# The Toeplitz stage of a hybrid state-space and attention layer in steps of four groups

## The chip, the cores and the metric

The kernel runs on one core of a Trainium2 chip. The metric is the device time of one execution in microseconds (us). A core has five engines that matter here: TensorE (PE in the profile, with its weight loads as PEld), VectorE (DVE), ScalarE (ACT), GpSimd (POOL) and SyncE (SP, which here only issues transfers). Each works through its own queue of instructions in order; they wait for each other through semaphores. Sixteen DMA engines move data between the chip's memory (DRAM) and the on-chip SBUF; transfers are issued from the queues of SP, ACT and POOL. TensorE writes its results to PSUM, in banks of 128 x 512 numbers of 32 bits.

## What is computed

One encoder layer over two sequences of 512 tokens with 1024 channels: an S5 state-space branch and a windowed attention branch are gated and added, then comes a squared-ReLU MLP. The change is in the S5 branch, which for 64 groups of 16 channels runs a complex linear recurrence of 64 states forward and backward and reads the states out:

```python
def one_direction(us, d, reverse):
    bu_re = jnp.einsum('lgc,gpc->lgp', us, bb_re[d])
    bu_im = jnp.einsum('lgc,gpc->lgp', us, bb_im[d])
    ...
    _, _, h_re, h_im = lax.associative_scan(_complex_combine, (ar, ai, bu_re, bu_im),
                                            reverse=reverse, axis=0)
    return (jnp.einsum('lgp,gcp->lgc', h_re, cr[d])
            - jnp.einsum('lgp,gcp->lgc', h_im, ci[d]))

y = one_direction(ug, 0, False) + one_direction(ug, 1, True)
y = jax.nn.gelu(y + dsk * uf)
return y * jax.nn.sigmoid(y @ w_glu + b_glu)
```

Queries, keys, values, the branch's input `u` and two gates come from one projection `h @ w_in`. Everything is in 32-bit floating point.

## The kernel before

**The recurrence in chunks.** A sequence is cut into 64 chunks of T = 8 tokens (NCHUNK = 64). Inside a chunk the output is a Toeplitz product of the inputs; between chunks a state `h` is handed on by a scan of 62 iterations on DVE (L600 to L606). The output of a group is then three products that add up in one area of 128 x 128 in PSUM: the Toeplitz matrix `toep` by the input `u_sb` (L642), and the table `ctab` (real and imaginary part) by the chunk states `st` (L645).

**The tables stage before it** (`tables`, L464 to L566) makes for every four groups a table of nine powers, 9 x 16 columns for each part, and writes it to DRAM (`ct_scr`, L522, from POOL's queue). The ninth power serves only the lag products of that stage; the Toeplitz stage uses the first T x 16 columns. `toep_scr` is written in DRAM as well (L576).

**The Toeplitz stage** (L594 to L668) takes the 64 groups in 32 steps q of two groups (SH = 2). The order of a step is written out by hand for TensorE, ACT and DVE (`manual_schedule`, L599: these three run in the order of the program); POOL and SP are placed by a planner. In step q:

1. TensorE: products of both groups into one PSUM bank `ps` from a pool of two banks (`sps`, L639 to L646).
2. The state copies for step q + 2 (`state_rows`, L609 to L618): rows 64 to 127 on DVE, rows 0 to 63 on ACT for an even q and on DVE for an odd one; three buffers of tag `st`.
3. DVE: `remainder()` of step q - 1, the lower part `ylo` = `yg` - `yhi` (L622).
4. In every second step ACT issues the two stores of the four groups before (`store_y`, L626: `yhi`, then `ylo`).
5. ACT: GELU of the bank into `yg` (L655) and its rounding `yhi` (L621).
6. `pull(n)`: filler matmuls, see below.
7. POOL: the loads of a new table every four groups (`load_table`, L590, three buffers) and of `u_sb` and `toep` every eight groups (`load_batch`, L582 and L584, two buffers each).

A bank is written again two steps later, and only when the GELU has read it.

**Fillers.** While DVE and ACT do the scan and these steps, TensorE works off other products of the layer: `pull(n)` (L260) takes matmuls from a generator until n units are used up. First come 24 columns of the projection (`products` and `column`, L180 to L212; each in two halves, one for a sequence, of 24 matmuls, two units a matmul), then eight key tiles (`key_products`, L214 to L239; 24 matmuls of one unit each). Together that is 2 x 3 x 8 x 2 x 24 + 3 x 8 x 8 = 2496 units. What belongs to a product is written into the queues at the place where it is pulled:

- the last matmul of a half brings `finish`: ACT copies the result out of PSUM (L200 here), and after a column's second half ACT issues its store (L209);
- the 4th and the 10th matmul of a column's first half, and the 3rd and the 7th of the first key tile, bring `split`: ACT rounds a piece of the next weights to `c_hi` (L175), DVE makes the remainder `c_lo` (L176);
- the last matmul of a key tile brings a chain: square on ACT (L232), sum on DVE (L234), addition and power on POOL (L236, L237), multiplication on DVE (L238).

In the Toeplitz stage the units that are left are spread evenly over the steps (L660), but for 84, which are pulled after its end (L667) before the attention begins with `w_lo` (L981) and its first product (L813).

```python
pull(32)                                             # L608
...
pull(-(-(phase["units"] - 84) // (GROUPS // SH - q)))  # L660
```

Of the kernel before, what the change touches and what calls it, by code (L numbers as in the profile page):

```python
# [12 lines left out]
F32 = mybir.dt.float32  # L13
F32R = mybir.dt.float32r
I32 = mybir.dt.int32
AF = mybir.ActivationFunctionType
# [3 lines left out]
P = 128  # L20
# [5 lines left out]
NSEQ = 2  # L26
# [12 lines left out]
GROUPS = 64  # L39
STATE = 64  # L40
CH = 16
T = 8
NCHUNK = SEQ // T
SB = 8
SI = 4
SG = 4
SH = 2
# [16 lines left out]
def hybrid_layer(ctx, tc, x, rel, onehot, w_qkv, w_ug, vectors, lam, coefs, w_glu, w_out, ln2,  # L64
                 w_up, w_down, out):
    nc = tc.nc
    V, S, PE, GP, SP = nc.vector, nc.scalar, nc.tensor, nc.gpsimd, nc.sync
# [4 lines left out]
    dram = ctx.enter_context(tc.tile_pool(name="dram", bufs=1, space=DRAM))  # L72
# [22 lines left out]
    ga_scr = dram.tile([KT, P, NTOK], F32, name="ga_scr")  # L95
# [55 lines left out]
    phase = {"next": 0, "raw": [], "units": 2 * 3 * KT * NSEQ * len(columns) + 3 * KT * NT, "gelu": False}  # L151
# [119 lines left out]
    with tc.tile_pool(name="xin", bufs=1, reuse_waits="tile") as xin, tc.tile_pool(name="ssmc", bufs=1) as sc:  # L271
# [148 lines left out]
        ps = ps_o.tile([P, 512], F32, tag="po", name="line")  # L420
# [21 lines left out]
    with tc.tile_pool(name="hst", bufs=1) as hp:  # L442
# [11 lines left out]
        with tc.tile_pool(name="ssmt", bufs=2) as sp:  # L454
# [9 lines left out]
            def tables(c):  # L464
# [22 lines left out]
                for q in range(SB // SG):  # L487
                    g0 = c * SB + q * SG
# [20 lines left out]
                    for ri, t in enumerate((bi_p, br_p)):  # L509
# [5 lines left out]
                    ctab = sp.tile([P, SG, 2, 9, CH], F32, tag="ctab", name="ctab")  # L515
# [3 lines left out]
                    V.tensor_sub(ctab[:, :, 0], tb, ctab[:, :, 0])  # L519
                    V.tensor_mul(ctab[:, :, 1], bc_pow(er, 9), bc_ch(cw[:, 1], 9))  # L520
                    V.tensor_sub(ctab[:, :, 1], ctab[:, :, 1], tb)
                    GP.dma_start(ct_scr[:, g0:g0 + SG].rearrange("p g r n -> p (g r n)"),  # L522
                                 ctab.rearrange("p g r n c -> p (g r n c)"))


                    u_sb = sp.tile([P, SI, NSEQ * NCHUNK], F32, tag="u_sb", name="u_sb", bufs=1)
                    SP.dma_start(u_sb, u_scr[g0:g0 + SI].rearrange("g c t k -> (c t) g k"))
                    bms = []
                    for gp in range(SG // SH):
                        bm = sp.tile([P, 2, SH, P], F32, tag="bm", name="bm")  # L530
                        bms.append(bm)
                        ps = tps()
# [45 lines left out]
        with tc.tile_pool(name="ssmo", bufs=2) as sp:  # L578
            def load_batch(g0):

                u_sb = sp.tile([P, SB, NSEQ * NCHUNK], F32, tag="u_sb", name="u_sb")
                GP.dma_start(u_sb, u_scr[g0:g0 + SB].rearrange("g c t k -> (c t) g k"))  # L582
                toep = sp.tile([P, SB, T, CH], F32, tag="toep", name="toep")
                GP.dma_start(toep.rearrange("p g t c -> p g (t c)"),  # L584
                             toep_scr[:, :, g0:g0 + SB].rearrange("c t g n -> (c t) g n"))
                return u_sb, toep

            def load_table(g0):
                ctab = sp.tile([P, SI, 2, 9 * CH], F32, tag="ctab", name="ctab_in", bufs=3)
                GP.dma_start(ctab.rearrange("p g r n -> p (g r n)"),  # L590
                             ct_scr[:, g0:g0 + SI].rearrange("p g r n -> p (g r n)"))
                return ctab

            ahead = [load_batch(0)]  # L594
            ahead_c = [load_table(0), load_table(SI), load_table(2 * SI)]
            ahead.append(load_batch(SB))
            GP.dma_start(line_scr, line_one[:, None, :].to_broadcast([N_HEADS, P, LINE]))
            order.close()
            order.enter_context(tc.manual_schedule(engines={mybir.EngineType.PE, mybir.EngineType.Activation, mybir.EngineType.DVE}))  # L599
            for i in range(1, NCHUNK - 1):  # L600
                t1, t2 = [sp.tile([P, 2, GROUPS, NSEQ], F32, tag="st", name=n, bufs=3) for n in ("t1", "t2")]
                V.tensor_mul(t1, h[:, i], a8r)
                V.tensor_mul(t2, h[:, i, ::-1], a8i)
                V.tensor_add(t1, t1, h[:, i + 1])
                V.tensor_add(h[:, i + 1], t1, t2)
                pull(15)  # L606
            phase["gelu"] = True
            pull(32)  # L608
            def state_rows(q):  # L609
                st = sp.tile([P, 2, SH, NSEQ, NCHUNK], F32, tag="st", name="st", bufs=3)  # L610
                hv = h[:, :, :, q * SH:(q + 1) * SH, :].rearrange("p k r g s -> p r (g s) k")
                sv = st.rearrange("p r g s k -> p r (g s) k")
                V.tensor_copy(sv[64:128], hv[64:128, :, :, ::-1])
                if q % 2 == 0:
                    S.copy(sv[0:64], hv[0:64])
                else:
                    V.tensor_copy(sv[0:64], hv[0:64])
                return st  # L618

            def rounded(y, parts, g):  # L620
                S.copy(parts[0][:, g:g + SH, :], y)  # L621
                return lambda: V.tensor_sub(parts[1][:, g:g + SH, :], y, parts[0][:, g:g + SH, :].bitcast(F32))  # L622

            def store_y(parts, ga):
                for e in range(2):
                    S.dma_start(y_scr[e, :, :, ga:ga + SI].rearrange("t c g k -> (t c) (g k)"),  # L626
                                parts[e].rearrange("p g k -> p (g k)").bitcast(F32))

            states = [state_rows(0), state_rows(1)]
            remainder = full = None  # L630
            for q in range(GROUPS // SH):
                g0 = q * SH
                if g0 % SB == 0:
                    u_sb, toep = ahead.pop(0)
                if g0 % SI == 0:
                    ctab = ahead_c.pop(0)
                    ysp = [sp.tile([P, SI, NSEQ * NCHUNK], F32R, tag=f"y{n}", name=f"y{n}") for n in ("hi", "lo")]
                st = states.pop(0)
                ps = sps()  # L639
                for g in range(SH):  # L640
                    o = ps[:, g * P:(g + 1) * P]
                    PE.matmul(o, toep[:, g0 % SB + g].rearrange("p t c -> p (t c)"), u_sb[:, g0 % SB + g, :],  # L642
                              start=True, stop=False)
                    for ri in range(2):
                        PE.matmul(o, ctab[:, g0 % SI + g, ri, 0:T * CH],  # L645
                                  st[:, ri, g].rearrange("p s k -> p (s k)"), start=False, stop=ri == 1)  # L646
                if q + 2 < GROUPS // SH:
                    states.append(state_rows(q + 2))
                if remainder:
                    remainder()  # L650
                if full:
                    store_y(*full)
                    full = None
                yg = sp.tile([P, SH, NSEQ * NCHUNK], F32, tag="yg", name="yg")
                S.activation(yg.rearrange("p g k -> p (g k)"), ps[:, 0:SH * P], AF.Gelu_apprx_tanh)  # L655
                remainder = rounded(yg, ysp, g0 % SI)
                if (g0 + SH) % SI == 0:
                    full = ysp, g0 + SH - SI

                pull(-(-(phase["units"] - 84) // (GROUPS // SH - q)))  # L660
                if (g0 + SH) % SI == 0 and g0 + SH + 2 * SI < GROUPS:
                    ahead_c.append(load_table(g0 + SH + 2 * SI))
                if (g0 + SH) % SB == 0 and g0 + SH + SB < GROUPS:
                    ahead.append(load_batch(g0 + SH + SB))
            remainder()
            store_y(*full)
            pull(phase["units"])  # L667
            order.close()  # L668
# [67 lines left out]
    with tc.tile_pool(name="att", bufs=2, reuse_waits="tile") as ap, tc.tile_pool(name="attc", bufs=1, reuse_waits="tile") as ac:  # L736
# [289 lines left out]
        with tc.manual_schedule(engines={ET.PE, ET.Activation, ET.DVE, ET.Pool}):  # L1026
            for i, (j, sq) in enumerate(steps):
# [149 lines left out]
    with tc.tile_pool(name="glu", bufs=1, reuse_waits="tile") as gpool, \  # L1177
# [4 lines left out]
        for u in range(2, 2 * KT):  # L1182
            m, s = divmod(u, 2)
# [160 lines left out]
    with tc.tile_pool(name="up", bufs=2, reuse_waits="tile") as fp:  # L1344
# [43 lines left out]
        for r in range(NPAIR):  # L1388
# [41 lines left out]
    with tc.tile_pool(name="downb", bufs=1, side="right", reuse_waits="tile") as db, \  # L1430
# [47 lines left out]
        ps = product_d(1)  # L1478
# [5 lines left out]
        ps = product_d(5)  # L1484
# [5 lines left out]
        ps = product_d(6)  # L1490
# [3 lines left out]
        ps = product_d(3)  # L1494
# [4 lines left out]
        ps = product_d(7)  # L1499
# [5 lines left out]
        ps = product_d(2)  # L1505
# [3 lines left out]
        ps = product_d(4)  # L1509
# [82 lines left out]
```

## Time and profile before

| what | value |
|---|---|
| median of 3 runs | 1488.72 us (1487.78 to 1491.35) |
| profiled execution | 1487.76 us |
| its span in the profile | 1486.0 us |
| matmuls, busy | 8074, 1447.0 us (97%) |
| ScalarE, VectorE, GpSimd busy | 761.0, 1102.7, 209.8 us |
| scan on DVE | 212.9 to 323.4 us |
| Toeplitz products, first to last start | 326.8 to 411.4 us |
| GELU, 128 x 256 | 32 times, 384 ns median |
| state copy, 64 x 512, DVE and ACT | 774 and 1090 ns median |

The profile shows one execution. A row of a group gives engine, operation, output and inputs with their shapes, the count, then busy time and mean time of one, then the idle time of the engine ahead of it with what ended it. In rows in order of time the first number is the start in us from the span's beginning, the second the length, and a bracket the engine's idle time with what ended it. ACTq and POOLq are the issuing parts of these engines. TensorE's matmuls overlap, so the distance of their starts tells more than their lengths; products of 32-bit numbers appear as two matmul records each in the Toeplitz stage (128 and 256 records for 64 and 128 products).

### The profile page before, as it was taken

Reading aid. Unit: us, or ns where it says so; the run is one execution under the profiler, and the core shown is the slowest. Engines: PE = TensorE matmul, PEld = TensorE weight load, DVE = VectorE, ACT = ScalarE, POOL = GpSimd, SP = SyncE. Lnnn points to the kernel's source line nnn. Section 1 sums busy time; section 2 is a strip of 40 time slices with the busy share of each in tenths; the row PEclk is TensorE's granted clock in tenths of the full one; section 3 lists DMA queues with packets and bytes.
Section 4 is the critical chain, followed back from the end, with each engine's and each line's share of the span. In section 5 each row is a group of like instructions: output and inputs, shape, how many; then the busy total and the mean of one; then the engine's idle time right before and its main releaser. Section 6 shows DMA issues by size and latency. Waiting matters only on the chain.

```text
span 1486.0 us, 22128 instructions
## 1 busy us (share of the span) xinstructions
PE 1447.0 (97%) x8074; PEld 1230.8 (83%) x8074; DVE 1102.7 (74%) x1989; ACT 761.0 (51%) x1362; POOL 209.8 (14%) x372
## 2 busy tenths in 40 slices
PE   6999999999999999999999989999999999999998
PEld 4788888878999999998777868888888878888787
DVE  7998859976645899988965578777776588575553
ACT  6777752226535888785433345544444443333332
POOL 3133351002232444221100000000000000000000
PEclk9999999999999999999999999999999999999999
DMA  4455459229840545376543234444443894454441
GB/s 175 141 171 170 162 180 367 107 85 326 321 155 15 165 142 179 100 263 207 184 150 132 87 131 149 153 149 156 154 151 128 309 334 128 155 174 153 128 128 57
DMA packets 103165, 249.69 MB, mean 168 GB/s; under 512 B 12266, under 2 KB 23786, under 8 KB 103056
## 3 DMA queue, kind: packets, MB, share of 16 engines
q1 hardware_dynamic: 60528, 140.07, 29.1%
q0 software_dynamic: 16896, 53.53, 10.4%
q10 hardware_dynamic: 25632, 54.67, 9.8%
q8 instruction: 64, 1.05, 0.3%
q14 instruction: 45, 0.37, 0.1%
HBM read 173.74 MB, written 90.21 MB: 178 GB/s over the span
## 4 chain that ended last, share of the span: by engine, by line
PE 84%; DVE 6%; ACT 4%; DMA 3%; issue 3%; POOL 1%; ACTq 0%; SPq 0%; DVEq 0%; POOLq 0%
PE acc L185 14%; PE bank L117 13%; PE bank L118 13%; PE bank L116 13%; PE acc L813 6%; PE acc L123 4%; PE po L896 3%; PE sps L864 2%; PE tps L880 2%; PE acc L117 2%; PE acc L118 2%; PE acc L116 2%; PE sps L547 2%; PE acc L835 1%; DMA toep<-toep_scr 1%
## 5 line engine op out<-in xcount | busy, mean ns | idle before, releaser
L185 PE MATMUL acc<-act,c_hi 128*128 128x512 f32 x768 | 250.2, 401 | 1.0 <-DVE act L304 1.0
L117 PE MATMUL bank<-b_lo,a_hi 128*128 128x512 f32 x448 | 174.8, 390 | 1.4 <-DVE b_lo L1461 1.4
L118 PE MATMUL bank<-b_hi,a_lo 128*128 128x512 f32 x448 | 174.3, 389 | 0.0
L116 PE MATMUL bank<-b_hi,a_hi 128*128 128x512 f32 x448 | 173.5, 389 | 0.0
L185 PEld LDWEIGHTS acc<-act,c_hi 128*128 128x128 f32 x768 | 142.6, 190 | 29.2 <-DVE act L304 2.4
L185 PE MATMUL acc<-act,c_lo 128*128 128x512 f32 x384 | 153.2, 399 | 0.0
L1460 ACT CAST a_hi<-d_a 128x1024 fp32r<-128x1024 f32 x56 | 59.0, 1054 | 179.9 <-PE bank L117 176.5
L116 PE MATMUL bank<-act,act 128*128 128x512 f32 x368 | 144.0, 391 | 4.9 <-ACT act L1350 4.9
L117 PE MATMUL bank<-act,act 128*128 128x512 f32 x368 | 143.8, 391 | 0.0
L118 PE MATMUL bank<-act,act 128*128 128x512 f32 x368 | 143.7, 390 | 0.0
L1461 DVE TENSOR_TENSOR a_lo<-d_a,a_hi 128x1024 fp32r<-128x1024 f32 x56 | 68.4, 1222 | 100.0 <-ACT a_hi L1460 100.0
L813 PE MATMUL acc<-w_hi,act 128*128 128x256 f32 x512 | 114.2, 291 | 0.0
L117 PEld LDWEIGHTS bank<-b_lo,a_hi 128*128 128x128 f32 x448 | 84.1, 188 | 20.3 <-DVE b_lo L1461 3.0
L116 PEld LDWEIGHTS bank<-b_hi,a_hi 128*128 128x128 f32 x448 | 84.1, 188 | 17.6
L118 PEld LDWEIGHTS bank<-b_hi,a_lo 128*128 128x128 f32 x448 | 84.1, 188 | 17.3
L813 PEld LDWEIGHTS acc<-w_hi,act 128*128 128x128 f32 x512 | 87.1, 189 | 3.7
L116 PEld LDWEIGHTS bank<-act,act 128*128 128x128 f32 x368 | 69.5, 189 | 19.8 <-ACT act L1350 5.3
L185 PEld LDWEIGHTS acc<-act,c_lo 128*128 128x128 f32 x384 | 72.8, 190 | 14.0 <-DVE c_lo L176 0.4
L123 PE MATMUL acc<-act,gc_hi 128*128 128x512 f32 x256 | 81.1, 394 | 1.5 <-ACT gc_hi L683 1.5
L118 PEld LDWEIGHTS bank<-act,act 128*128 128x128 f32 x368 | 69.4, 189 | 14.9 <-DVE act L1351 0.4
L117 PEld LDWEIGHTS bank<-act,act 128*128 128x128 f32 x368 | 69.5, 189 | 14.3
L874 ACT ACTIVATE p<-p,nmx 128x257 f32<-128x257 f32 (+1 forms) x128 | 72.1, 564 | 17.9 <-DVE nmx L868 16.7
(328 smaller groups left out, 3420.0 us busy)
## 6 DMA issues: line engine op xcount, KB each, us to landing
d_a<-a_scr SPq DMA_DIRECT2D x56, 512.0 KB, 3.6
u_raw<-in_w_up_dram SPq DMA_DIRECT2D x32, 512.0 KB, 5.2
a_scr<-t ACTq DMA_DIRECT2D x64, 256.0 KB, 4.9
k<-in_w_down_dram SPq DMA_DIRECT2D x32, 512.0 KB, 6.7
c_raw<-in_w_ug_dram SPq DMA_DIRECT2D x48, 256.0 KB, 3.6
a_scr<-a ACTq DMA_DIRECT2D x46, 256.0 KB, 2.1
ct_scr<-ctab POOLq DMA_DIRECT2D x16, 576.0 KB, 3.8
ctab_in<-ct_scr POOLq DMA_DIRECT2D x16, 576.0 KB, 7.4
```

The lines of the kernel that those rows point to most:

```text
L116: PE.matmul(ps, a[0], b[0], start=first, stop=False)
L117: PE.matmul(ps, a[0], b[1], start=False, stop=False)
L118: PE.matmul(ps, a[1], b[0], start=False, stop=last)
L123: PE.matmul(ps, w[wi][:, k, :], rows[yi], start=k + p == 0, stop=k == KT - 1 and p == 2)
L185: PE.matmul(ps, w[wi][:, k, :], hT[s][hi][:, k, :], start=n == 0, stop=n == 3 * KT - 1)
L547: PE.matmul(ps[:, i * P:(i + 1) * P], bm[:, ri, g, :], u_sb[:, gp * SH + g, :], start=True, stop=True)
L813: PE.matmul(self.ps, hT[sq][act][:, k, col:col + P], w[:, k % 4, :], start=i == 0, stop=i == 3 * KT - 1)
L864: PE.matmul(ps[:, 0:self.nk], qs, kk[:, self.k0 * P:self.k1 * P], start=i == 0, stop=i == 1)
L874: S.activation(p, p, AF.Exp, bias=self.nmx[:, h:h + 1], scale=-1.0, accum_out=self.sums[:, h, self.qb:self.qb + 1])
L896: PE.matmul(self.po, vv, self.hl[i][part], start=i + part == 0, stop=i == self.nkb - 1 and part == 1)
L1460: S.copy(hi, src)
L1461: V.tensor_sub(lo, src, hi.bitcast(F32))
```

## The change

The Toeplitz stage runs in 16 steps b of four groups (SI = 4). A step computes its products in both banks one after the other. Then comes half of its filler matmuls, then the state copies for the step after it, the lower parts and the store of the step before it, GELU and rounding of both banks, and the other half of the fillers. Inputs and Toeplitz matrices are loaded by four groups into four buffers (by eight into two before), `toep` ahead of `u_sb`; the tag `st` has four buffers instead of three; the table is written to DRAM without the ninth power; and the pull ahead of the stage is 48 units instead of 32.

```diff
-    ct_scr = dram.tile([P, GROUPS, 2, 9 * CH], F32, name="ct_scr")
+    ct_scr = dram.tile([P, GROUPS, 2, T * CH], F32, name="ct_scr")
...
-                    GP.dma_start(ct_scr[:, g0:g0 + SG].rearrange("p g r n -> p (g r n)"),
-                                 ctab.rearrange("p g r n c -> p (g r n c)"))
+                    GP.dma_start(ct_scr[:, g0:g0 + SG].rearrange("p g r n -> p (g r) n"),
+                                 ctab[:, :, :, 0:T].rearrange("p g r n c -> p (g r) (n c)"))
...
-                u_sb = sp.tile([P, SB, NSEQ * NCHUNK], F32, tag="u_sb", name="u_sb")
-                GP.dma_start(u_sb, u_scr[g0:g0 + SB].rearrange("g c t k -> (c t) g k"))
-                toep = sp.tile([P, SB, T, CH], F32, tag="toep", name="toep")
+                toep = sp.tile([P, SI, T, CH], F32, tag="toep", name="toep", bufs=4)
                 GP.dma_start(toep.rearrange("p g t c -> p g (t c)"),
-                             toep_scr[:, :, g0:g0 + SB].rearrange("c t g n -> (c t) g n"))
+                             toep_scr[:, :, g0:g0 + SI].rearrange("c t g n -> (c t) g n"))
+                u_sb = sp.tile([P, SI, NSEQ * NCHUNK], F32, tag="u_sb", name="u_sb", bufs=4)
+                GP.dma_start(u_sb, u_scr[g0:g0 + SI].rearrange("g c t k -> (c t) g k"))
...
-                ctab = sp.tile([P, SI, 2, 9 * CH], F32, tag="ctab", name="ctab_in", bufs=3)
+                ctab = sp.tile([P, SI, 2, T * CH], F32, tag="ctab", name="ctab_in", bufs=3)
...
-            ahead.append(load_batch(SB))
+            ahead += [load_batch(i * SI) for i in range(1, 4)]
...
-            pull(32)
+            pull(48)
...
-                st = sp.tile([P, 2, SH, NSEQ, NCHUNK], F32, tag="st", name="st", bufs=3)
+                st = sp.tile([P, 2, SH, NSEQ, NCHUNK], F32, tag="st", name="st", bufs=4)
...
+            left, full = [], None
+            for b in range(GROUPS // SI):
+                g0 = b * SI
+                u_sb, toep = ahead.pop(0)
+                ctab = ahead_c.pop(0)
+                ysp = [sp.tile([P, SI, NSEQ * NCHUNK], F32R, tag=f"y{n}", name=f"y{n}") for n in ("hi", "lo")]
+                banks = []
+                for q in range(SI // SH):
+                    st = states.pop(0)
+                    ps = sps()
+                    banks.append(ps)
+                    for g in range(SH):
+                        o, k = ps[:, g * P:(g + 1) * P], q * SH + g
+                        PE.matmul(o, toep[:, k].rearrange("p t c -> p (t c)"), u_sb[:, k, :], start=True, stop=False)
+                        for ri in range(2):
+                            PE.matmul(o, ctab[:, k, ri, 0:T * CH],
+                                      st[:, ri, g].rearrange("p s k -> p (s k)"), start=False, stop=ri == 1)
+                pulled = -(-(phase["units"] - 84) // (GROUPS // SI - b))
+                pull(pulled // 2)
+                if g0 + SI < GROUPS:
+                    states += [state_rows((g0 + SI) // SH + q) for q in range(SI // SH)]
+                for rest in left:
+                    rest()
+                if full:
+                    store_y(*full)
+                left = []
+                for q, ps in enumerate(banks):
+                    yg = sp.tile([P, SH, NSEQ * NCHUNK], F32, tag="yg", name="yg")
+                    S.activation(yg.rearrange("p g k -> p (g k)"), ps[:, 0:SH * P], AF.Gelu_apprx_tanh)
+                    left.append(rounded(yg, ysp, q * SH))
+                full = ysp, g0
+                pull(pulled - pulled // 2)
+                if g0 + 3 * SI < GROUPS:
+                    ahead_c.append(load_table(g0 + 3 * SI))
+                if g0 + 4 * SI < GROUPS:
+                    ahead.append(load_batch(g0 + 4 * SI))
```

The loop over q (L630 to L666), whose order is given above, goes.

More of the change, by code (lines that the diff above doesn't have):

```diff
@@ L600, in hybrid_layer @@
             for i in range(1, NCHUNK - 1):
-                t1, t2 = [sp.tile([P, 2, GROUPS, NSEQ], F32, tag="st", name=n, bufs=3) for n in ("t1", "t2")]
+                t1, t2 = [sp.tile([P, 2, GROUPS, NSEQ], F32, tag="st", name=n, bufs=4) for n in ("t1", "t2")]
                 V.tensor_mul(t1, h[:, i], a8r)
@@ L629, in hybrid_layer @@
             states = [state_rows(0), state_rows(1)]
[L630 to L650, printed above, removed]
+            left, full = [], None
@@ L651, in hybrid_layer @@
                 if full:
                     store_y(*full)
[L653 to L662, printed above, removed]
@@ L663, in hybrid_layer @@
-                if (g0 + SH) % SB == 0 and g0 + SH + SB < GROUPS:
-                    ahead.append(load_batch(g0 + SH + SB))
-            remainder()
+                left = []
[4 more added lines that the diff above has]
+                full = ysp, g0
@@ L666, in hybrid_layer @@
+                pull(pulled - pulled // 2)
[3 more added lines that the diff above has]
+                    ahead.append(load_batch(g0 + 4 * SI))
+            for rest in left:
+                rest()
             store_y(*full)
```

## The prediction

> **What bounds the kernel now.** I read the page first, then the busy time by stretch for the stage that the change touches, then the order of time of each engine in it.
>
> ```profile
> span 1486.0 us, 22128 instructions
> PE 1447.0 (97%) x8074; PEld 1230.8 (83%) x8074; DVE 1102.7 (74%) x1989; ACT 761.0 (51%) x1362; POOL 209.8 (14%) x372
> ```
> ```profile
> 212.00:322.00 110.00, 110.00 (x487) 91.13 (x486) 104.53 (x265) 24.00 (x41) 11.62 (x16) 1.00 0.58 208
> 329.00:332.40 3.40, 3.36 (x14) 3.07 (x15) 0.00 (x0) 3.31 (x5) 0.00 (x0) 0.56 0.10 37
> 345.00:400.00 55.00, 52.88 (x392) 49.14 (x391) 34.97 (x59) 31.07 (x61) 16.37 (x25) 1.00 1.01 360
> 878.60:882.10 3.50, 3.19 (x7) 2.32 (x8) 3.50 (x6) 0.88 (x2) 0.00 (x0) 0.55 0.00 0
> ```
> The columns are length, busy time and count of PE, weight loads, DVE, ACT and POOL, then clock, DMA share, GB/s. TensorE is the bound: no idle in the scan (110.00 of 110.00), and almost none in the Toeplitz stage, whose products start from 326.8 to 411.0 us (first row below). There the DMA engines are full too (1.01). So the stage can lose only its idle time, and that is small:
>
> ```profile
> L642 PE MATMUL sps<-u_sb,toep x128: 270/275/421, 326.8 to 411.0; 128*128 128x128 f32 x128
> ```
> ```profile
> L645 PE MATMUL sps<-st,ctab_in 128*128 128x128 f32 x256 | 39.9, 279 | 2.2 <-ACT st L615 1.8 <-DVE st L617 0.4
> L642 PE MATMUL sps<-u_sb,toep 128*128 128x128 f32 x128 | 25.3, 280 | 2.8 <-DMA toep<-toep_scr 1.9 <-ACT yg L655 0.8
> ```
> Five microseconds of idle in all. The first piece, 1.8, tells most (ACT, DVE, TensorE in order of time):
>
> ```profile
> 326.59 0.58 ACT L200 COPY sg<-acc 128x512 f32<-128x512 f32 x1 [4.84 <-PE acc L185]
> 327.21 0.33 ACTq L209 DMA_DIRECT2D gs_scr<-sg  x1
> 327.94 2.01 ACT L615 COPY st<-h 64x512 f32<-64x512 f32 x2 [0.76 <-ACT sg L200]
> ```
> ```profile
> 323.45 1.47 DVE L613 COPY st<-h 64x512 f32<-64x512 f32 x2
> ```
> ```profile
> 326.85 0.38 PE L642 MATMUL sps<-u_sb,toep 128*128 128x128 f32 x2
> 329.04 0.93 PE L645 MATMUL sps<-st,ctab_in 128*128 128x128 f32 x4 [1.81 <-ACT st L615]
> 335.51 0.38 PE L642 MATMUL sps<-u_sb,toep 128*128 128x128 f32 x2
> 336.76 0.70 PE L185 MATMUL acc<-act,c_hi 128*128 128x512 f32 x2
> 338.00 0.38 PE L642 MATMUL sps<-u_sb,toep 128*128 128x128 f32 x2
> ```
> ACT's state copy (1.0 each) needed nothing but the scan, over by 323.45, when DVE began its own halves. It stood in ACT's program order behind the `finish` of a filler column, which waited 4.84 us for TensorE. ACT and DVE run in written order here, so **an evacuation of a filler product holds back whatever is written behind it**. The wait also left the clock at 0.56 for 3.4 us, about 1.5 us more.
>
> **The same for a key product** (L232 to L238), whose chain crosses four engines:
>
> ```profile
> 402.95 0.38 ACT L232 ACTIVATE keys<-acc 128x256 f32<-128x256 f32 x1
> 406.96 0.33 ACTq L626 DMA_DIRECT2D y_scr<-ylo  x1
> 407.33 0.39 ACT L655 ACTIVATE yg<-sps 128x256 f32<-128x256 f32 x1 [3.00 <-DVE ylo L622]
> 408.06 0.38 ACT L655 ACTIVATE yg<-sps 128x256 f32<-128x256 f32 x1
> 408.90 0.33 ACTq L626 DMA_DIRECT2D y_scr<-yhi  x1
> ```
> ```profile
> 403.36 0.42 DVE L234 TENSOR_REDUCE ms<-keys 128x4 f32<-128x256 f32 x1 [0.36 <-ACT keys L232]
> 405.26 0.42 DVE L238 TENSOR_TENSOR keys<-acc,rk 128x256 f32<-128x256 f32 x1 [1.48 <-POOL rk L237]
> 405.70 0.77 DVE L613 COPY st<-h 64x512 f32<-64x512 f32 x1
> 406.50 0.43 DVE L622 TENSOR_TENSOR ylo<-yg,yhi 128x256 fp32r<-128x256 f32 x1
> ```
> ```profile
> 394.25 0.39 PE L642 MATMUL sps<-u_sb,toep 128*128 128x128 f32 x2
> 396.55 0.39 PE L642 MATMUL sps<-u_sb,toep 128*128 128x128 f32 x2
> 407.77 0.49 PE L642 MATMUL sps<-u_sb,toep 128*128 128x128 f32 x2 [0.84 <-ACT yg L655]
> 423.25 0.39 PE L813 MATMUL acc<-w_lo,act 128*128 128x256 f32 x1 [0.42 <-DVE w_lo L981]
> ```
> The square at 402.95 delays DVE's state copy to 405.70 (2.75 us), this delays `ylo`, this the store's issue, this the GELU at 407.33, and the GELU frees the bank for which TensorE waits at 407.77. Now the pull stands behind the GELU of its own step, and the next delayed one is needed over two steps (of 2.30 us) later; so the chain costs 0.84 at worst.
>
> **The change, part by part.** *Loads and tables.* Half-size loads go out a step earlier and `ctab_in` shrinks by a ninth (16 x 64 KB); the 1.9 us of waiting for `toep` goes. Splitting costs nothing:
>
> ```profile
> u_sb<-u_scr SPq DMA_DIRECT2D x16, 256.0 KB, 3.2
> u_sb<-u_scr POOLq DMA_DIRECT2D x8, 512.0 KB, 7.4
> ct_scr<-ctab POOLq DMA_DIRECT2D x16, 576.0 KB, 3.8
> ```
> Half the bytes land in less than half the time. POOL issues 16 more loads, and is 14% busy. The table store now goes in 512-byte runs and lands later than 3.8 us, at worst like `u_sb` in 7.4; its buffer has a second one and its readers come after 326 us: nothing. [...]
>
> *pull(48).* Eight more column matmuls (0.226 each, 110.00 over 487) come before the stage. But counted through, the `split`s of column 22 come with them: two `c_hi` on ACT, two `c_lo` on DVE, both ahead of the state copies.
>
> ```profile
> 335.29 0.62 ACT L175 CAST c_hi<-c_raw 128x512 fp32r<-128x512 f32 x1
> ```
> ```profile
> 335.93 0.69 DVE L176 TENSOR_TENSOR c_lo<-c_raw,c_hi 128x512 fp32r<-128x512 f32 x1 [0.69 <-ACT c_hi L175]
> 336.66 0.77 DVE L613 COPY st<-h 64x512 f32<-64x512 f32 x1
> ```
> TensorE arrives at 326.85 + 1.81 = 328.66. ACT: `sg` and store to 327.6, `c_hi` to 328.8; DVE: `c_lo` to 329.5, first upper half to 330.3, second state to 331.8. Idle: about 1.65, hardly below 1.81. Saving 0.2.
>
> *The pull split in two.* This is the part that decides. Step b is now: products in both banks, first half-pull, state copies for b+1, `ylo` and store of b-1, GELUs of b, second half-pull. A `finish`, `split` or key chain in the first half-pull stands ahead of the GELU of the same step, whose bank TensorE wants when the next step begins; one in the second half-pull has one step more.
>
> Where do they fall? Of 2496 units, 2084 are pulled by the scan's end (180 in the front, 128, 8 x 104 in the tables, 62 x 16), 412 remain: 110 column matmuls and 192 of keys. 24 go first; steps 0 to 8 take nine or ten, the later ones 16 of keys. Counting: **step 1**, first half: a finish. **Step 3**, second: finish and store; **step 4**, both: a split each. Step 6, second: a finish, as the half's first matmul, early enough. **Step 9**, first: finish, store, split; second: split. Keys 0 to 3: **step 10** second, **12** first, **13** second, 15 first.
>
> Prices. A step with ten fillers is 2 x 2.49 = 4.98 (335.51 to 338.00), with nine 4.75, with keys 2 x 2.30 = 4.60; products take 2 x 1.25 + 0.09 = 2.59. After a chain three state copies follow on DVE (2.3, three like 405.70), two `ylo` (0.42 + 0.46), issue to GELU 0.37, GELU to TensorE 0.44: 4.0. So from key square to free bank 2.75 + 4.0 = 6.74; from `c_hi` 1.37 (335.29 to 336.66) + 4.0 = 5.36; two GELUs with roundings 1.57 (407.33 to 408.90). Times count from the start of the step named (for key 0: of step 9).
> - Step 1: `sg` at 3.80 (2.59, four fillers, drain), 0.58 + state copy 1.0 + two issues with gaps 0.8 + 0.44: bank free at 6.6 against 4.98: **1.6**.
> - Steps 3, 4: `sg` at 4.71, store, `c_hi` at 5.70, free at 11.06 against 9.50: **1.6**. Next `c_hi` behind the GELUs at 10.62 + 1.57 = 12.19, free 17.55 against 15.81: **1.7**.
> - Step 9: `sg` at 3.35, `c_hi` 4.34, free 9.70 against 4.57: **5.1**. Second split at 10.83, free 16.19 against 14.30: **1.9**.
> - Key 0: square behind the GELUs at 15.75 + 1.57 = 17.32, free 24.06 against 20.79: **3.3**.
> - Key 1: square 3.37 into its step, free 10.11 against 4.60: **5.5**.
> - Key 2: square at 4.33, free 11.07 against 9.20: **1.9**. Key 3 delays no bank.
>
> Together 22.6. Between them no wait: without a chain DVE copies until 2.59 + 2 x 0.77 = 4.1, `ylo` is done at 5.0, as the next step begins, and a GELU may come 3 us late (bank 0 is ready at 1.3, wanted at 4.6 to 5.0). On POOL the loads wait only for products that are over when a key's two operations come; SP's loads keep their places.
>
> Off goes what was idle: 0.2 at the start, 1.9 `toep`, 0.4, 0.8: 3.3. Net 19.3.
>
> *Clock.* After 1.81 idle it fell to 0.56 for 3.4 us, after 4.91 to 0.55:
>
> ```profile
> 878.91 0.79 PE L116 MATMUL bank<-act,act 128*128 128x512 f32 x1 [4.91 <-ACT act L1350]
> ```
> Each fall costs some 1.5 us unless a later wait swallows it (after step 9). I count the idles of 3.3 and 5.5: 3.0; bounds none and six, 0 to 9. [...]
>
> *The end.* Key 4's square, held by step 15's GELUs, comes some 3.4 us later before the end of fillers than now; keys 5 to 7 give 1.4 back, and `w_lo` (0.42 waited for now) follows: 2 more, bounds 0 and 3.
>
> Sum: 19.3 + 3.0 + 2 = 24.3 on the profiled 1487.76 (span 1486.0 and 1.76 around it): 1512. The median of 1488.72 lies 1 above that execution; I leave 1512.
>
> **Rivals.** *A, faster: the queues don't hold.* If state copies, `ylo` and GELUs passed the waiting evacuations, as they would if the planner moved them, the stage would run at TensorE's pace: 1487.76 - 3.3 - 1.5 (clock) = 1483. The point is whether a key chain in step 12 stops DVE. Against it: 327.94 behind 326.59, and 405.70 behind 405.26.
> *B, no change: the DMA engines set the pace.* At 1.01 share, with only 1 MB fewer table bytes to read, TensorE's waits would sit under the loads' time: 1488. Against it: `toep` cost 1.9 us in all while the engines were full. Were half-size loads as slow as whole ones, the twelve later steps would each lose 7.4 - 3.2 = 4.2 us: 50, so 1538; the row with 3.2 speaks against that. [...]
> *C, slower, but half:* only finishes and splits wait (1.6 + 3.3 + 7.0) and key chains find slack that I overlook: 1487.76 + 11.9 - 3.3 + 1.5 = 1498.
> *D, more:* every wait drops the clock and `w_lo` comes 3 late: 1512 + 6 + 1 = 1519.
>
> **How the numbers follow.** Forecast 0.66, A 0.07, B 0.05 (0.01 of it the slow loads), C 0.12, D 0.10. About 0.3% (4.5 us) is what a measurement of this kernel can tell from no change. Predicted 1512; the range 1497 to 1520 takes in C and D and leaves out A and B. A makes faster by over 0.3% about 0.05 (1483 is just past it), same 0.06, slower 0.89.
>
> **What would show it.** Right: GELU waits for `ylo` of 3 us and more; TensorE idle of some 5 us twice, before the steps after 9 and 12, released by GELU; none by `toep`; granted clock below 1 after them; the stage about 20 us longer than 84. Wrong: state copies ahead of a key's multiply on DVE, TensorE idle on DMA, or a stage no longer than now.

## The result and the profile after

| | before | after |
|---|---|---|
| median, us (lowest to highest) | 1488.25 (1486.51 to 1491.35, 4 runs) | 1511.54 (1510.86 to 1514.44, 4 runs) |
| profiled execution, us | 1487.76 | 1510.86 |
| its span, us | 1486.0 | 1509.1 |
| mean granted clock | 0.998 | 0.992 |

The kernel became slower: ratio 1.0158, 95% interval 1.0142 to 1.0174, in a comparison of both on the same chip. The forecast was 1512.

The page of after starts with these lines:

```profile
span 1509.1 us, 22157 instructions
PE 1453.6 (96%) x8074; PEld 1237.7 (82%) x8074; DVE 1100.2 (73%) x1989; ACT 761.3 (50%) x1362; POOL 227.0 (15%) x388
```

The count of matmuls is the same (8074) and so is the work of every engine within a few microseconds. The span is 23.1 longer: that is waiting and clock, not work. The groups by line for the stretch 320 to 445 us put the waiting in one place (the last columns are the idle time of TensorE ahead of the group and what ended it):

```profile
L643 PE MATMUL sps<-u_sb,toep 128*128 128x128 f32 x128 | 27.9, 303 | 16.3 <-ACT yg L658 16.3
```

In before the same group (L642 there) had 2.8 us, 1.9 of it for a DMA. Now it has 16.3, all released by a GELU (L658), none by a load. In order of time, TensorE's rows of after with idle time ahead of them are these, from the first product to the attention branch (the bracket is the idle time and its releaser):

```profile
329.85 0.68 PE L645 MATMUL sps<-st,ctab_in 128*128 128x128 f32 x4 [1.40 <-ACT st L615]
340.44 0.49 PE L643 MATMUL sps<-u_sb,toep 128*128 128x128 f32 x2 [0.58 <-ACT yg L658]
356.34 0.49 PE L643 MATMUL sps<-u_sb,toep 128*128 128x128 f32 x2 [1.17 <-ACT yg L658]
362.45 0.49 PE L643 MATMUL sps<-u_sb,toep 128*128 128x128 f32 x2 [1.09 <-ACT yg L658]
386.11 0.76 PE L643 MATMUL sps<-u_sb,toep 128*128 128x128 f32 x2 [4.61 <-ACT yg L658]
399.61 0.62 PE L643 MATMUL sps<-u_sb,toep 128*128 128x128 f32 x2 [2.43 <-ACT yg L658]
411.10 0.79 PE L643 MATMUL sps<-u_sb,toep 128*128 128x128 f32 x2 [5.01 <-ACT yg L658]
424.75 0.49 PE L643 MATMUL sps<-u_sb,toep 128*128 128x128 f32 x2 [1.47 <-ACT yg L658]
437.38 0.39 PE L225 MATMUL acc<-c_hi,act 128*128 128x256 f32 x1 [0.58 <-DVE keys L238]
441.92 0.66 PE L797 MATMUL tps<-ident,kd 128*128 128x128 f32 x4 [1.41 <-POOL kd L788]
443.86 0.38 PE L815 MATMUL acc<-w_hi,act 128*128 128x256 f32 x1 [1.28 <-ACT w_hi L982]
445.30 0.58 PE L815 MATMUL acc<-w_lo,act 128*128 128x256 f32 x1 [1.05 <-DVE w_lo L983]
```

The seven rows from 340.44 to 424.75 are waits at the start of steps 2, 5, 6, 10, 12, 13 and 15: the steps that the prediction named, but for step 11. The one of 5.01, ahead of step 13, shows the mechanism whole. ACT in order of time, then DVE:

```profile
404.70 0.39 ACT L232 ACTIVATE keys<-acc 128x256 f32<-128x256 f32 x1 [3.98 <-PE acc L225]
404.71 0.33 ACTq L626 DMA_DIRECT2D y_scr<-yhi  x1
404.98 1.07 ACT L615 COPY st<-h 64x512 f32<-64x512 f32 x1
410.29 0.33 ACTq L626 DMA_DIRECT2D y_scr<-ylo  x1
410.66 0.39 ACT L658 ACTIVATE yg<-sps 128x256 f32<-128x256 f32 x1 [4.61 <-DVE ylo L622]
```
```profile
405.12 0.42 DVE L234 TENSOR_REDUCE ms<-keys 128x4 f32<-128x256 f32 x1 [6.34 <-ACT keys L232]
407.04 0.42 DVE L238 TENSOR_TENSOR keys<-acc,rk 128x256 f32<-128x256 f32 x1 [1.50 <-POOL rk L237]
407.48 1.37 DVE L613 COPY st<-h 64x512 f32<-64x512 f32 x2
408.86 0.73 DVE L617 COPY st<-h 64x512 f32<-64x512 f32 x1
409.51 0.75 DVE L622 TENSOR_TENSOR ylo<-yg,yhi 128x256 fp32r<-128x256 f32 x2
```

Read it backwards from 411.10. TensorE waits for the GELU at 410.66. ACT was free from 406.05 (404.98 + 1.07), but the store of `ylo` stands ahead of the GELU, and `ylo` was not there. DVE was free from 409.51 only, because three state copies stood ahead, and they stood behind the key multiply of 407.04, which waited 1.50 for POOL. None of these copies needs the key, and DVE had been idle for 6.34 us before the key's sum at 405.12. The answer by stretch for this wait and what follows it (columns as in the prediction):

```profile
404.00:411.00 7.00, 2.09 (x18) 1.89 (x16) 4.33 (x9) 1.69 (x3) 1.83 (x3) 0.93 0.38 112
411.00:415.00 4.00, 3.90 (x18) 3.90 (x19) 2.09 (x5) 2.92 (x7) 0.00 (x0) 0.50 0.55 201
```

In seven microseconds TensorE worked for 2.09, no engine was near full, and the DMA engines were at 0.38; then it ran at half clock.

**Where the 23.1 us lie.** Idle time of TensorE in the stage, from 329.85 to 437.38 above: 18.3; in before 5.0 (1.81, 1.9, 0.36, 0.84). That is +13.4. The last key product starts at 422.4 in before and at 440.2 in after, +17.8; the 4.4 between go with the slower clock, whose falls are priced below. From there to the first attention product it takes 0.1 us in before (422.4 to 422.5) and 3.7 in after (440.2 to 443.9): +3.6. The opening of the attention branch, up to the first product of L896 (L898 in after), takes 46.5 and 47.8 us: +1.3; here too the clock is at 0.50, from 444.20 to 451.03, which it is nowhere in this stretch of before. The rest is 0.4.

### The profile page after: what moved, and what is told of

Same layout as the page of the kernel before. It is cut to its first block, busy times and chain, and to the rows that moved or that the text cites. A ratio compares the mean times of both kernels' runs of the same rounds, so it can differ in the third digit from the quotient of the medians.

```text
span 1509.1 us, 22157 instructions
## 1 busy us (share of the span) xinstructions
PE 1453.6 (96%) x8074; PEld 1237.7 (82%) x8074; DVE 1100.2 (73%) x1989; ACT 761.3 (50%) x1362; POOL 227.0 (15%) x388
## 4 chain that ended last, share of the span: by engine, by line
PE 83%; DVE 7%; ACT 4%; DMA 2%; issue 2%; POOL 1%; ACTq 0%; SPq 0%; DVEq 0%; POOLq 0%
PE acc L185 14%; PE bank L117 13%; PE bank L118 13%; PE bank L116 13%; PE acc L815 5%; PE acc L123 4%; PE po L898 2%; PE sps L866 2%; PE acc L117 2%; PE acc L118 2%; PE acc L116 2%; PE tps L882 2%; PE sps L547 2%; PE sps L645 2%; PE acc L837 1%
## 5 line engine op out<-in xcount | busy, mean ns | idle before, releaser
L185 PE MATMUL acc<-act,c_hi 128*128 128x512 f32 x768 | 249.5, 399 | 1.0 <-DVE act L304 1.0
L185 PEld LDWEIGHTS acc<-act,c_hi 128*128 128x128 f32 x768 | 142.5, 189 | 29.6 <-DVE act L304 2.4
L185 PE MATMUL acc<-act,c_lo 128*128 128x512 f32 x384 | 151.9, 396 | 0.0
L185 PEld LDWEIGHTS acc<-act,c_lo 128*128 128x128 f32 x384 | 72.4, 188 | 14.1 <-DVE c_lo L176 0.5
```

Source lines behind the costliest of these rows:

```text
L185: PE.matmul(ps, w[wi][:, k, :], hT[s][hi][:, k, :], start=n == 0, stop=n == 3 * KT - 1)
```

## The experiments

Eight kernels were run. The first four below shared one comparison, in which before had a median of 1488.52; the last four another, with 1487.82. Five start from after, three from before. The theory: evacuations of filler products, written ahead of state copies, lower parts, stores and GELUs, hold these back. The rivals: the smaller loads and their bandwidth; the step of four groups as such, with two banks held together.

**The pull behind the GELUs.** After, without the first half-pull:

```diff
-                pull(pulled // 2)
...
-                pull(pulled - pulled // 2)
+                pull(pulled)
```

> The changed kernel with the whole pull of a step behind its GELUs. Queue order (my theory): no evacuation stands ahead of the GELU of its own step any more, so the waits of 4.6 and 5.0 us go; counted through, key chains and splits still reach the next step late three times by 1.4 to 2.8. TensorE idle in the stage some 10 us (18.3 in the changed kernel), two falls of the clock: 1499 us (1494 to 1503). Step size (rival: the doubled block of three state copies, two lower parts and two stores is too long for two banks wherever the fillers stand): 1506 or more. DMA engines: no difference, 1511.

Measured: 1495.58 (1493.33 to 1496.57), ratio 1.0049 [1.0033, 1.0064]. So 16.0 of the 23.3 us between the medians hang on where the fillers are written. TensorE's two longest waits are now

```profile
392.40 0.49 PE L643 MATMUL sps<-u_sb,toep 128*128 128x128 f32 x2 [2.48 <-ACT yg L657]
...
411.80 0.49 PE L643 MATMUL sps<-u_sb,toep 128*128 128x128 f32 x2 [2.48 <-ACT yg L657]
```

With 1.42, 1.09, 1.20 and 0.64 they make 9.3 in the stage. Loads, tables, banks and the size of a step are those of after. The last three (2.48, 0.64, 2.48) are key chains: they now have a step's products more before a bank is wanted, which is not enough. The 1.42 is the first state copy, 1.09 and 1.20 are splits. The clock fell once in the stage (0.53 from 393.00 to 396.50), not twice as expected.

**The pull ahead of everything.** After, with all fillers in the first place: the same edit turned round.

```diff
-                pull(pulled // 2)
+                pull(pulled)
...
-                pull(pulled - pulled // 2)
```

> The changed kernel with the whole pull of a step ahead of state copies and GELUs: the suspected cost doubled. Queue order: every evacuation now stands ahead of the GELU of its own step; waits of 6.6, 5.4 and 6.3 at keys 0 to 2, 6.0 and 4.7 at the finishes with splits, 1 to 2 three times more, some 33 us of idle and five falls of the clock: 1529 us (1520 to 1538). Step size and DMA engines: no difference, 1511.

Measured: 1535.60 (1532.05 to 1537.07), ratio 1.0312 [1.0297, 1.0327]. Keys 0 to 2 now cost 6.43, 5.23 and 6.05, nearly the whole length of a chain; the two longest waits:

```profile
405.69 0.80 PE L643 MATMUL sps<-u_sb,toep 128*128 128x128 f32 x2 [6.43 <-ACT yg L658]
...
435.83 0.80 PE L643 MATMUL sps<-u_sb,toep 128*128 128x128 f32 x2 [6.05 <-ACT yg L658]
```

The expectation had 6.6, 5.4, 6.3, 6.0 and 4.7 for five of them; measured 6.43, 5.23, 6.05, 5.79 and 4.41. The idle time in the stage is 32.6 (some 33 expected). The time came out 6.6 us above the expected value; the clock fell five times in the stage, as expected, but four of these falls lasted over 3.5 us (0.50 throughout 392.70 to 396.20, 406.00 to 409.50, 423.00 to 426.50 and 436.20 to 439.70; the other gave 0.63 from 359.70 to 363.20), and the mean granted clock of the execution was 0.984 against 0.992 in after. The same matmuls in three places give 1495.6, 1511.5 and 1535.6: the place decides.

**The loads alone.** Before, with loads of four groups in four buffers, `toep` first, and tables without the ninth power; steps stay at two groups:

```diff
+    ct_scr = dram.tile([P, GROUPS, 2, T * CH], F32, name="ct_scr")
...
+                toep = sp.tile([P, SI, T, CH], F32, tag="toep", name="toep", bufs=4)
...
+                u_sb = sp.tile([P, SI, NSEQ * NCHUNK], F32, tag="u_sb", name="u_sb", bufs=4)
...
+            ahead += [load_batch(i * SI) for i in range(1, 4)]
```

> The kernel before with the loads alone: four groups in four buffers, the Toeplitz matrix first, the table without the ninth power; steps and pulls as before. Queue order: only the 1.9 us of TensorE idle on the Toeplitz load go, 1486.5 us (1485 to 1488), idle in the stage 3.0 instead of 5.0. DMA engines as the bound: 2.4 us or more off, since 0.83 MB less has to be read in the full stretch, and a DMA share below 1 there. Split loads too slow: slower than before.

Measured: 1488.05 (1485.04 to 1492.87), ratio 0.9999 [0.9988, 1.001]: no difference, and just outside the expected range. The loads neither cost nor bring anything that can be seen by themselves, though the DMA share from 345 to 400 us went from 1.01 to 0.95. All of TensorE's waits from the first product to the last:

```profile
327.30 0.71 PE L644 MATMUL sps<-st,ctab_in 128*128 128x128 f32 x4 [1.81 <-ACT st L615]
...
386.73 0.49 PE L641 MATMUL sps<-u_sb,toep 128*128 128x128 f32 x2 [0.42 <-ACT yg L654]
394.94 0.71 PE L644 MATMUL sps<-st,ctab_in 128*128 128x128 f32 x4 [0.84 <-DVE st L617]
403.12 0.49 PE L641 MATMUL sps<-u_sb,toep 128*128 128x128 f32 x2 [0.98 <-ACT yg L654]
```

The 1.9 us of waiting for `toep` have gone, as predicted. But the waits for later state copies and GELUs grew from 1.2 (0.36, 0.84) to 2.2, perhaps because ACT and DVE had caught up where TensorE waited for a load; no run tests that reason. The sum fell from 5.0 to 4.1 only, not to 3.0 as expected: too little to measure.

**The keys late.** After, with a key's sum, power and multiply kept back: the square stays in its place, the sum is issued behind the GELUs of the step and the multiply one step after that.

```diff
+            def sums(kt=kt, psv=psv):
...
+                return lambda: V.tensor_mul(kt, psv, rk[:, :, None].to_broadcast([P, N_KV, HD]))
...
+                owing.append(sums)
...
+                settle()
                 pull(pulled - pulled // 2)
```

> The changed kernel with the sum, the power and the multiplication of a key tile written into the queues one and two steps later, behind the GELUs; only the square stays in its place. Queue order: the waits of 2.4, 5.0 and 1.5 us at the keys shrink to 0.7 at most and their falls of the clock go, the wait of 4.6 at the finish and split of step 9 stays: 1498 us (1495 to 1502). Step size: the blocks are as long as before, 1509 or more.

Measured: 1496.58 (1496.11 to 1499.12), ratio 1.0057 [1.0043, 1.0071]. Of the two longest waits of after (4.61 and 5.01), one is left:

```profile
387.46 0.54 PE L655 MATMUL sps<-u_sb,toep 128*128 128x128 f32 x2 [4.60 <-ACT yg L670]
403.43 0.49 PE L655 MATMUL sps<-u_sb,toep 128*128 128x128 f32 x2 [0.30 <-ACT yg L670]
427.60 0.66 PE L813 MATMUL tps<-ident,kd 128*128 128x128 f32 x4
428.53 0.38 PE L831 MATMUL acc<-w_hi,act 128*128 128x256 f32 x1 [0.27 <-ACT w_hi L998]
```

The 4.60 ahead of step 10 comes from a `finish` and a `split`, which this edit does not touch, and it stayed to a hundredth; the key waits (2.43, 5.01, 1.47) shrank to 0.30. So both kinds hold the queues, as the prediction had it, and rival C (half) falls. From the last key product (427.27) to the first attention product it takes 1.26, not 3.7 as in after, with the key transposes ahead of it in both. So by this run some 2.4 of the 3.6 at the hand-over belong to the late key chains and 1.2 to the order.

**The first state copies ahead of the pull.** Before, with one thing changed: the copies that the first two steps need are written ahead of `pull(32)`.

```diff
-            pull(32)
...
+            states = [state_rows(0), state_rows(1)]
+            pull(32)
```

> The kernel before with the first two state copies written ahead of the pull that leads to the stage, nothing else. Queue order: the copies no longer stand behind the finish of a filler column, the first wait of 1.8 us goes and with it the fall of the clock where it follows: 1486 us (1485 to 1487). If the wait had another cause (the scan's end, the table load on ACT): no change, 1488.5.

Measured: 1486.74 (1482.28 to 1491.68), ratio 0.9993 [0.9979, 1.0007]: no measurable difference. The 1.81 has gone, so ACT's copy did stand behind the `finish` for nothing. The time went into the loads:

```profile
349.18 0.76 PE L643 MATMUL sps<-u_sb,toep 128*128 128x128 f32 x2 [2.44 <-DMA toep<-toep_scr]
372.30 0.46 PE L643 MATMUL sps<-u_sb,toep 128*128 128x128 f32 x2 [1.40 <-DMA toep<-toep_scr]
393.68 0.46 PE L643 MATMUL sps<-u_sb,toep 128*128 128x128 f32 x2 [1.97 <-DMA toep<-toep_scr]
```

1.9 of waiting for `toep` in before became 5.8, with 0.92 for a GELU behind it. This is one execution, of 1490.72 us, 4.0 above the median of this kernel, so the waits for loads may be shorter in most of the others. Together with the loads alone it suggests that the stage of before has two limits close together, and that taking away either shows the other; it does not prove it.

**Both mends of the queues.** After, with the pull behind the GELUs and the keys late.

```diff
-                pull(pulled // 2)
...
-                pull(pulled - pulled // 2)
+                settle()
+                pull(pulled)
```

> The changed kernel with both mends: the whole pull behind the GELUs, and sum, power and multiplication of a key tile one and two steps later. Queue order: the waits at the keys go, those at splits of 1.1 and 1.2 us and the first of 1.4 stay, and steps of four groups cost nothing by themselves: 1488 us (1486 to 1491). Step size: some of the 7 us by which the pull behind the GELUs alone is slower than before stays, 1492 or more.

Measured: 1484.69 (1482.60 to 1488.34), ratio 0.9978 [0.9965, 0.9992], below the expected range of 1486 to 1491. Idle in the stage: 1.41, 1.11 and 1.20, and no fall of the clock in it (in an execution of 1488.34, the longest of the ten). The whole loss of the change is undone, and a little more, with its banks, loads, buffers and step size in place: the rival that blames the size of a step falls.

**All mends.** The same, and the first state copies ahead of `pull(48)`.

```diff
-            pull(48)
...
+            states = [state_rows(0), state_rows(1)]
+            pull(48)
```

> The same with the first state copies ahead of the pull that leads to the stage as well: 1.4 us off the kernel with both mends, 1486 to 1487 us by the queue order. Step size: as in the kernel with both mends.

Measured: 1483.60 (1481.67 to 1484.98), ratio 0.9967 [0.9955, 0.998]. The 1.41 is gone; 1.12 and 1.20 are left. The gain on both mends is 1.1 with overlapping intervals (1.4 expected); the time lies below the expected 1486 to 1487, since the kernel it starts from did.

**The mends with steps of two groups.** Before's loop, with the loads and tables of after, the first copies ahead of `pull(32)`, and the keys late.

```diff
+            states = [state_rows(0), state_rows(1)]
+            pull(32)
...
+                toep = sp.tile([P, SI, T, CH], F32, tag="toep", name="toep", bufs=4)
...
+                owing.append(sums)
...
+                settle()
```

> The kernel before in its steps of two groups, with the small loads and table, the first state copies ahead of the pull, and the key chains one and two steps later. Queue order: none of the waits of 1.81, 0.42, 0.84 and 0.98 us that the kernel with the loads alone shows is left: 1484 us (1482.5 to 1486), below both kernels. Step size: the same, since the steps are short. DMA engines: 1487 or more.

Measured: 1482.02 (1479.68 to 1486.35), ratio 0.9958 [0.9942, 0.9974]: the fastest of all, some 6 us below before and 0.5 below the expected range. One wait is left among the products, where none was expected:

```profile
389.75 0.49 PE L654 MATMUL sps<-u_sb,toep 128*128 128x128 f32 x2 [0.39 <-ACT yg L667]
```

Its distance from the version with steps of four is 1.6 us with overlapping intervals, so steps of four groups bring nothing that can be seen here, and cost little once the queues are free. The loads and the early copies, neither of which shows a gain alone, are in this kernel beside the late keys. No run has the late keys alone in steps of two groups, or loads and early copies together without them, so how the 5.8 us divide among the three is not shown.

## Why the prediction was right, point by point

**The mechanism** was as predicted and is shown, not only argued: moving the pull either way (1495.6 and 1535.6) and taking the keys' chain out (1496.6) move the time and the named waits. Rival A (queues that don't hold) falls by the rows at 404.70 to 410.66. Rival B (DMA sets the pace) falls by the loads alone, at 0.9999, and by the missing DMA releasers in after. C falls by the keys-late run. D asked for every wait to drop the clock; those of 1.40, 0.58, 1.17, 1.09 and 1.47 did not. Its other half, an end 3 us late, came about (below).

**The waits, one by one:**

| ahead of step | 2 | 5 | 6 | 10 | 11 | 12 | 13 | 15 | sum |
|---|---|---|---|---|---|---|---|---|---|
| predicted, us | 1.6 | 1.6 | 1.7 | 5.1 | 1.9 | 3.3 | 5.5 | 1.9 | 22.6 |
| measured, us | 0.58 | 1.17 | 1.09 | 4.61 | 0 | 2.43 | 5.01 | 1.47 | 16.4 |

The counting of fillers, by which the steps were found, held. (The pulls in its brackets add up to 2132, not 2084; the 110 column matmuls left are right: before has 73 + 37 L185 matmuls that end after 323.45.) The sizes were too large, for three reasons. First, chains were added up operation by operation. From key square to TensorE the prediction had 6.74; the rows give 6.40 (404.70 to 411.10); from `c_hi` 5.36, measured 5.00 (381.11 to 386.11). Copies that follow each other on DVE overlap: three took 2.03 (407.48 to 409.51), not 2.3, and two `ylo` 0.78, not 0.88. Second, on ACT a store's issue stands in a queue of its own beside the copy. Step 1 in after:

```profile
338.54 0.59 ACT L200 COPY sg<-acc 128x512 f32<-128x512 f32 x1 [5.07 <-PE acc L185]
338.55 0.33 ACTq L626 DMA_DIRECT2D y_scr<-yhi  x1
338.91 0.44 ACTq L626 DMA_DIRECT2D y_scr<-ylo  x1
339.02 1.09 ACT L615 COPY st<-h 64x512 f32<-64x512 f32 x1
340.02 0.37 ACT L658 ACTIVATE yg<-sps 128x256 f32<-128x256 f32 x1
```

Both issues pass within the time of evacuation and copy, so from `sg` to the free bank it takes 1.90 (338.54 to 340.44) and not 0.58 + 1.0 + 0.8 + 0.44 = 2.82. Where ACT did wait for an issue, the data was late, as `ylo` at 410.29. Third, the wait ahead of step 11 was swallowed: after the 4.61, step 10 ran at a low clock and took 6.32 (386.11 to 392.43) instead of 4.60, which hid the second split, whose GELU came at 391.71. The prediction had allowed that for the clock, not for the wait.

**The start.** `pull(48)`: 1.65 predicted, 1.40 measured. The prediction named the `split` that comes with the pull, and it is there; the gain of 0.4 on 1.81 is small either way: taking the whole wait away, with the early copies, made no measurable difference.

**The loads.** No wait for `toep`, as predicted. But the reason given was wrong. It read from two rows that half the bytes land in less than half the time; one row was of SP's queue, the other of POOL's. In after, POOL's own loads of half the size are

```profile
toep<-toep_scr POOLq DMA_DIRECT2D x16, 256.0 KB, 5.4
u_sb<-u_scr POOLq DMA_DIRECT2D x16, 256.0 KB, 6.6
```

`u_sb` took 6.6 against 7.4 for twice the bytes (7.9 with the loads alone); `toep`, now issued ahead of it, 5.4 against 9.2. By the prediction's side rival, loads as slow as whole ones would have cost 4.2 in each of twelve steps. `u_sb` was nearly as slow, and it cost nothing: these loads go out three steps ahead, and no cost of splitting reached TensorE (0.9999 for the loads alone). So the prediction was right to count none, but its two rows did not show it. The table store landed in 4.1 us against 3.8, later, as predicted.

**The clock.** 3.0 predicted, 4.4 measured in the stage, as the difference of two sums. It fell after 4.61, 2.43 and 5.01 (386.18 to 389.59, 399.83 to 403.24, 410.07 to 416.90); before's fall after 1.81 (329.39 to 332.80) has no counterpart after 1.40. In after a window of 3.41 us at 0.50 held 18 matmuls (399.83 to 403.24) and one at 1.00 held 32 (389.59 to 393.00). Put at half of the time that TensorE was busy in the falls (3.41, 3.41 and 5.80 us), the loss is 1.7, 1.7 and 2.9, less 1.7 for before's (3.41 busy): an estimate of 4.6. The prediction had two falls of 1.5 and no fall of double length.

**The end.** 2 predicted with bounds of 0 and 3; the hand-over took 3.6, the idle ahead of the key products 0.58, and the opening of attention 1.3 more: 5.5. This is the step that failed in its bounds. The opening also ran at half clock for 6.83 us, which its sum did not have. The prediction let `w_lo` follow the keys by itself; but in after the key transposes (L797) stand ahead of the first attention product, and `w_hi` behind their evacuation on ACT:

```profile
442.62 0.69 ACT L798 ACTIVATE kh<-tps,vec 128x512 fp32r<-128x512 f32 x1 [1.68 <-PE tps L797]
443.20 3.21 ACT L982 CAST w_hi<-w_in 128x512 fp32r<-128x512 f32 x6
```

In before `w_hi` (420.15) went ahead between two key squares (419.87 and 422.75). It is the same mechanism once more, one stage later: an evacuation that waits holds what is written behind it. Why the program has another order there was not tried; with the pull behind the GELUs the transposes follow the attention product again.

**The sum.** Waits came out 6.2 smaller than predicted and the start 0.25; clock, end and rest came out 1.4, 3.5 and 0.4 larger: 24.3 - 6.4 + 5.3 = 23.2, against 23.1 measured. That 1512 met 1511.5 so closely is owed to errors of both signs; the range of 1497 to 1520 was what the argument could support. Of its signs, one was off: the Toeplitz products, from first to last start, took 98.9 us, some 15 longer than the 84 of before and not 20; the rest of the loss lies behind them.

## What to carry to other kernels

When filler work on the busiest engine is to be spread more evenly, follow not the filler but its evacuation: it stands in the written order of the other engines, and it holds back everything behind it until the filler is done, so write it behind what the next step needs. Price such a chain from the first waiting instruction to the one that frees the bank, count in whole filler units where each falls, and take away the longest first. And where two edits that each take a wait away by the trace each measure nothing, they may be covering each other: here the smaller loads and the early copies each did, and the kernel with both and the late keys gained 0.4%, though no run shows which of the three it needs.

## What the runs showed of the hardware

The granted clock has two values in the traces of before and after, 1 and 0.5. Every fall ahead of the end of these two executions lasts 3.41 or 6.83 us, and within a trace the falls start whole multiples of 3.413 us apart: in after at 386.18, 399.83, 410.07, 444.20 and 901.59, which is 4, 7, 17 and 151 times 3.413 behind the first; in before at 329.39 and 878.93, which is 161 times. A window below is a stretch of 3.413 us, counted from the falls of its trace.

The length of an idle time does not tell whether the clock falls: of two equal waits of 2.48 with the pull behind the GELUs, one had a fall behind it and one had none. These are windows of that trace, each with the one behind it:

```profile
389.49:392.90 3.41, 0.93 (x8) 0.72 (x7) 3.36 (x6) 0.91 (x3) 0.97 (x2) 1.00 1.02 366
392.90:396.31 3.41, 3.41 (x18) 3.41 (x18) 1.48 (x4) 2.35 (x5) 0.00 (x0) 0.50 0.80 290
...
409.97:413.38 3.41, 1.58 (x14) 1.58 (x15) 1.84 (x5) 1.48 (x4) 0.00 (x0) 1.00 0.21 79
413.38:416.79 3.41, 3.41 (x32) 3.41 (x31) 0.42 (x1) 1.87 (x5) 0.28 (x2) 1.00 0.52 190
```

The first wait (389.92 to 392.40) lies in one window, in which TensorE worked for 0.93 us; the next window ran at 0.50, with 18 matmuls. The second (409.32 to 411.80) is cut by the edge at 409.97; 1.58 us of work were left in its second window, and the next one ran at 1.00, with 32 matmuls. Likewise the 1.81 at the start lay in one window in before (325.97 to 329.39), with 1.61 us of work, and the next ran at 0.50; with the loads alone the clock was 1.00 behind the same 1.81 (328.50 to 332.00). The 1.40 of after lay in a window with 2.01 us of work (328.15 to 331.56), and no fall followed. Short waits in one window add up: at the hand-over of after none is longer than 1.41, but together they leave 0.99 us of work.

```profile
440.79:444.20 3.41, 0.99 (x5) 0.60 (x5) 1.39 (x4) 1.73 (x4) 2.49 (x5) 1.00 0.00 0
444.20:447.61 3.41, 2.36 (x12) 2.32 (x12) 3.41 (x7) 2.21 (x5) 0.00 (x0) 0.50 0.73 233
```

Counted over the windows of before and after from 60 to 1470 us, seven falls begin. Six windows at full clock had less than 1.6 us of work (0.00, 0.00, 0.02, 0.07, 0.98 and 0.99), and each was followed by a fall. Of 15 with 1.61 to 2.45 us one was, that of 1.61 in before; of 794 with more, none. Two falls went on into a second window, where TensorE was busy for 2.38 and 2.36 us of the first; all seven ended behind a window with 3.15 us or more.

What exactly is counted stays open: 1.58 us of work once left the clock at 1 and 1.61 once did not, and the ends of matmuls are modelled in a profile.
